# Gathered rows dealt to the sixteen partition sets in one unbroken count, with the half-loaded batch among them

## The chip, the core and the metric

The kernel runs on one core of a Trainium2 chip. Five engines of the core work side by side: TensorE (PE, with its weight loads shown as PEld), VectorE (DVE), ScalarE (ACT), GpSimd (POOL) and SyncE (SP). Each takes its instructions in program order, and waits on semaphores for the others. Data moves between the device's memory and the on-chip memory by DMA: a transfer over 128 partitions is spread over sixteen DMA engines. The metric is device time in microseconds (us); less is better.

## What is computed

For each of 32 batches, 128 rows of 1024 floats are picked out of 512 by an index list:

```python
x:       (32, 512, 1024) float32
indices: (32, 128) int32, values 0..511
for b in range(batch):
    result[b] = x[b, indices[b]]
```

The indices are drawn from a fixed seed. A batch names between 109 and 120 different rows with its 128 indices; the rest are repeats. A row is 4 KB, so the output is 16.8 MB, and reading every named row once would be about 14.9 MB.

## The kernel before

A batch can go one of three ways to the output.

**Direct batches.** The first HEAD = 4 batches are gathered as they are: one indirect DMA on POOL's queue fetches row indices[b, p] into partition p of a block (repeats are read again), and a store on SP's queue writes the block out. TensorE takes no part. The loop over range(HEAD) issues them, after the columns of indices have been turned upright (idxT, by one product of vf with ident).

**Sparse batches.** Batches 5 to 31 are read without repeats. For each, the kernel finds which of the 128 positions are the first with their value, numbers these, gives each number a partition, and fetches only these rows into a buffer of the ring held (RING = 8 buffers u0 to u7, zeroed by ScalarE at the start). Entries that get no row point beyond the batch and are skipped by the bounds check. A product with a 0/1 matrix (spread[b]) then copies the fetched rows to all the positions that want them, in two halves of 512 columns (spread_rows); ScalarE copies the halves from PSUM to the block, and SP stores it. When TensorE is done with a buffer, the gather for eight batches later is issued to it (fetch).

The index work is done for GROUP = 3 batches at once, in three steps:
- step0 (lines 166 to 175): a product spreads each batch's values over all partitions (bc); VectorE counts for each position the earlier positions with the same value (cnt) and marks those with none (lead).
- step1 (177 to 187): a product of lead with the triangle above counts the leaders before each position (rk, then nth). An exclusive-or with shift, which is the batch's number modulo 16, changes which sets get the odd rows. The result, made unusable for non-leaders by 256 x cnt, is compared with turn to give the matrix pack.
- step2 (189 to 198): a product with pack puts each leader's index on its partition (at, the table that the gather reads), and a comparison with bc gives the spreading matrix.

turn comes from rank, which is laid out so that the low four bits of a number name one of sixteen sets of eight neighbouring partitions. Thus a batch with 112 + r different rows gives each set seven rows, and r of the sets an eighth.

**The half-loaded batch.** Batch 4 (HALF) has its rows 0 to 255 loaded whole at the start by two plain DMAs on ScalarE's queue (early). Only its indices from 256 up are gathered, each at its own position and with repeats (half_index), into ring buffer u0. half_spread makes its own bc and three matrices: one for each early tile and the identity for u0. half_rows adds the products, the early ones in the opening and the last one when spread_rows(4) runs.

**Order.** Program order on PE, DVE and ACT is kept by the wrapper InOrder. In the opening come half_index and the fetch of batch 4; step0 of groups 0 and 1; then for four groups step1, step0 of the next group but one (for g = 1 and 2), step2, and the fetches of batches up to 11. half_spread stands behind group 0, and the early halves of half_rows behind groups 1 and 2. The main loop goes over batches 4 to 31: spread_rows, the fetch for eight batches on, and one step of the group four ahead. The gathers of POOL's queue are thus issued in batch order, and so are the stores of SP's.

Of the kernel before, what the change touches and what calls it, by code (L numbers as in the profile page):

```python
# [6 lines left out]
F32 = mybir.dt.float32  # L7
F16 = mybir.dt.float16
I32 = mybir.dt.int32
ALU = mybir.AluOpType  # L10
# [18 lines left out]
def kernel(ctx, tc, x, indices, out):  # L29
# [11 lines left out]

    nc = tc.nc
    B, S, D = x.shape
    N = indices.shape[1]
    HEAD, RING, GROUP, AHEAD, FAR = 4, 8, 3, 4, 1024
    HALF = HEAD
    PAIRED = range(12, 20)  # L50
    SPARSE = HEAD + 1
    GROUPS = (B - SPARSE) // GROUP
    assert 2 * N <= S <= FAR and (B - SPARSE) % GROUP == 0
    const = ctx.enter_context(tc.tile_pool(name="const", bufs=1))
    ring = ctx.enter_context(tc.tile_pool(name="ring", bufs=1))
    rows = ctx.enter_context(tc.tile_pool(name="rows", bufs=1))
    pick = ctx.enter_context(tc.tile_pool(name="pick", bufs=1))
    junkp = ctx.enter_context(tc.tile_pool(name="junk", bufs=4))
    PS = bass.MemoryType.PSUM
    pbc = ctx.enter_context(tc.tile_pool(name="pbc", bufs=2, space=PS))  # L60
    psm = ctx.enter_context(tc.tile_pool(name="psm", bufs=1, space=PS))
    pout = ctx.enter_context(tc.tile_pool(name="pout", bufs=4, space=PS))
    pe, dve, act = InOrder(tc), InOrder(tc), InOrder(tc)
    mm, v = nc.tensor.matmul, nc.vector
# [8 lines left out]
    diff = const.tile([N, N], I32, name="diff")  # L73
    nc.gpsimd.iota(diff[:], pattern=[[1, N]], base=0, channel_multiplier=-1)
    rank = const.tile([N, 8, 16], I32, name="rank")
    for e in range(8):
# [2 lines left out]
            fold ^= col * (e >> bit & 1)  # L79
        steps = [[(-16 if fold >> bit & 1 else 16) << bit, 2] for bit in (2, 1, 0)]  # L80
        nc.gpsimd.iota(rank[:, e], pattern=[[1, 2]] + steps, base=2 * e + 16 * fold, channel_multiplier=0)
    shift = const.tile([N, 2, 16], I32, name="shift")
    nc.gpsimd.iota(shift[:], pattern=[[0, 2], [1, 16]], base=0, channel_multiplier=0)
    shift = shift[:].rearrange("p t s -> p (t s)")

    zero = const.tile([N, 1], F32, name="zero")
    dve(v.memset, zero[:], 0.0)
    ident = const.tile([N, B], F16, name="ident")
# [2 lines left out]
    dve(v.tensor_scalar, out=below[:], in0=diff[:], scalar1=0, scalar2=None, op0=ALU.is_lt)  # L91
    above = const.tile([N, N], F16, name="above")
    dve(v.tensor_scalar, out=above[:], in0=diff[:], scalar1=0, scalar2=None, op0=ALU.is_gt)
    turn = const.tile([N, N], F16, name="turn")
    dve(v.tensor_copy, out=turn[:], in_=rank[:].rearrange("p e q -> p (e q)"))
    vf = const.tile([N, N], F16, name="vf")
    dve(v.memset, vf[:], 0.0)
    dve(v.tensor_copy, out=vf[:B],
        in_=vals[:].bitcast(I32).rearrange("p (n two) -> p n two", two=2)[:, :, 0])
# [3 lines left out]
    early = [rows.tile([N, D], F32, name=f"early{k}") for k in range(2)]  # L103
# [10 lines left out]
    idxT = const.tile([N, B], I32, name="idxT")  # L114
    dve(v.tensor_copy, out=idxT[:], in_=tr[:])
    idxF = const.tile([N, B], F32, name="idxF")
# [6 lines left out]
    def gather(dst, at, b, **kw):  # L123
        nc.gpsimd.indirect_dma_start(  # L124
            out=dst, out_offset=None,
            in_=xf[:], in_offset=bass.IndirectOffsetOnAxis(ap=at, axis=0),
            element_offset=b * S * D, **kw)
# [22 lines left out]
    def table(name, dtype):  # L150
        return const.tile([N, B], dtype, name=name)

    cnt, lead, slot = table("cnt", F32), table("lead", F16), table("slot", F16)
    nth, at = table("nth", I32), table("at", I32)
    bcs, packs, spread = {}, {}, {}

    def of_group(g):
        return range(SPARSE + g * GROUP, SPARSE + (g + 1) * GROUP)

    def cols(t, g):  # L160
        return t[:, SPARSE + g * GROUP:SPARSE + (g + 1) * GROUP]

    def wide(t):
        return t.rearrange("p (g o) -> p g o", o=1).to_broadcast([N, GROUP, N])

    def step0(g):

        bcs[g] = bc = pbc.tile([N, 4, N], F32, name="bc")
        for k, b in enumerate(of_group(g)):
            pe(mm, bc[:, k], lhsT=ident[:, b:b + 1].to_broadcast([N, N]), rhs=vf[:], start=True, stop=True)  # L170
        for k, b in enumerate(of_group(g)):
            junk = junkp.tile([N, N], F16, name="junk")
            dve(v.scalar_tensor_tensor, out=junk[:], in0=bc[:, k], scalar=idxF[:, b:b + 1], in1=below[:],
                op0=ALU.is_equal, op1=ALU.mult, accum_out=cnt[:, b:b + 1])
        dve(v.tensor_scalar, out=cols(lead, g), in0=cols(cnt, g), scalar1=0.0, scalar2=None, op0=ALU.is_equal)

    def step1(g):

        rk = psm.tile([N, GROUP], F32, name="rk")
        pe(mm, rk[:], lhsT=above[:], rhs=cols(lead, g), start=True, stop=True)  # L180
        dve(v.tensor_copy, out=cols(nth, g), in_=rk[:])
        dve(v.tensor_tensor, out=cols(nth, g), in0=cols(nth, g), in1=cols(shift, g), op=ALU.bitwise_xor)
        dve(v.scalar_tensor_tensor, out=cols(slot, g), in0=cols(cnt, g), scalar=256.0, in1=cols(nth, g),
            op0=ALU.mult, op1=ALU.add)
        packs[g] = pack = junkp.tile([N, GROUP, N], F16, name="pack")
        dve(v.tensor_tensor, out=pack[:], in0=turn[:].rearrange("p (o n) -> p o n", o=1).to_broadcast([N, GROUP, N]),
            in1=wide(cols(slot, g)), op=ALU.is_equal)

    def step2(g):

        pos = psm.tile([N, GROUP], F32, name="pos")
        for k, b in enumerate(of_group(g)):
            pe(mm, pos[:, k:k + 1], lhsT=packs[g][:, k], rhs=near[:, b:b + 1], start=True, stop=True)
        dve(v.tensor_scalar, out=cols(at, g), in0=pos[:], scalar1=float(FAR), scalar2=None, op0=ALU.add)
        s = pick.tile([N, GROUP, N], F32, name=f"s{g}")
        dve(v.tensor_tensor, out=s[:], in0=bcs[g][:, :GROUP], in1=wide(cols(at, g)), op=ALU.is_equal)
        for k, b in enumerate(of_group(g)):
            spread[b] = s[:, k]

    def fetch(b):  # L200
        if HEAD <= b < B:
            gather(held[(b - HEAD) % RING][:], at[:, b:b + 1], b, bounds_check=S - 1, oob_is_err=False)

    held = []
# [2 lines left out]
        act(nc.scalar.copy, out=u[:], in_=zero[:].to_broadcast([N, D]))  # L207
        held.append(u)

    def half_index():  # L210

        c = slice(HALF, HALF + 1)
        dve(v.tensor_scalar, out=nth[:, c], in0=idxT[:, c], scalar1=2 * N, scalar2=FAR,
            op0=ALU.is_lt, op1=ALU.mult)
        dve(v.tensor_tensor, out=at[:, c], in0=nth[:, c], in1=idxT[:, c], op=ALU.add)

    def half_spread():

        less = const.tile([N, 1], F32, name="less")
        dve(v.tensor_copy, out=less[:], in_=diff[:, 0:1])  # L220
        bc = pbc.tile([N, 4, N], F32, name="bc")
        pe(mm, bc[:, 0], lhsT=ident[:, HALF:HALF + 1].to_broadcast([N, N]), rhs=vf[:], start=True, stop=True)
        same = pick.tile([N, 3, N], F32, name="same")
        for k in range(2):
            dve(v.tensor_scalar, out=same[:, k], in0=bc[:, 0], scalar1=less[:], scalar2=float(k * N),
                op0=ALU.add, op1=ALU.is_equal)
        dve(v.tensor_scalar, out=same[:, 2], in0=diff[:], scalar1=0, scalar2=None, op0=ALU.is_equal)
        spread[HALF] = same

    def half_rows(h, last):  # L230
        w = slice(h * 512, (h + 1) * 512)
        if not last:
            spread[HALF, h] = pout.tile([N, 512], F32, name="ps")
        ps, same = spread[HALF, h], spread[HALF]
        for k in ((2,) if last else (0, 1)):
            pe(mm, ps[:], lhsT=same[:, k], rhs=(early + held[:1])[k][:, w], start=k == 0, stop=k == 2)
        if last:
            nc.scalar.copy(out=blocks[HALF][:, w], in_=ps[:])  # L238

    def spread_rows(b):  # L240
        for h in range(2):
            if b == HALF:
                half_rows(h, True)
                continue
            w = slice(h * 512, (h + 1) * 512)
            ps = pout.tile([N, 512], F32, name="ps")
            pe(mm, ps[:], lhsT=spread[b], rhs=held[(b - HEAD) % RING][:, w], start=True, stop=True)
            nc.scalar.copy(out=blocks[b][:, w], in_=ps[:])  # L248
        store(b)

    half_index()
    fetch(HALF)
    step0(0)
    step0(1)
    for g in range(AHEAD):
        step1(g)
        if 0 < g < AHEAD - 1:
            step0(g + 1)
        step2(g)
        for b in of_group(g):  # L260
            if b < HEAD + RING:
                fetch(b)
        if g == 0:
            half_spread()
        elif g < 3:
            half_rows(g - 1, False)
    for b in range(HEAD, B):
        spread_rows(b)
        fetch(b + RING)
        g, step = divmod(b - SPARSE, GROUP)  # L270
        if b >= SPARSE and g + AHEAD < GROUPS:
            (step0, step1, step2)[step](g + AHEAD)


# [28 lines left out]
```

## Time and profile before

| | |
|---|---|
| median of 5 runs | 88.29 us (87.72 to 88.64) |
| the profiled execution | 89.93 us, of which the span is 88.1 us |
| busy in the span: PE / ACT / POOL / DVE | 63.0 / 41.8 / 33.8 / 27.5 us |
| DMA traffic | 32.86 MB, mean 373 GB/s |
| queue of POOL (gathers) | 14.96 MB |
| queue of SP (index loads and stores) | 16.81 MB |
| queue of ACT (early) | 1.05 MB |
| gathers to blocks / to the ring | 4 / 28 |

The span is the time from the first to the last instruction of one profiled execution. The page cuts it into 40 slices of 2.2 us and gives for each the busy share of every engine, the TensorE clock that was granted, the busy share of the DMA engines and what they moved. The chain of waits goes back from the last instruction to what released it, step by step. The timeline lists instructions with their start and duration, and in square brackets how long the engine had been idle and what ended that. A group such as "x4" is several instructions of one kind shown as one; a float32 product of 128x512 stands there as two matmuls. The time of a gather on POOL is that of issuing it; the rows land later. The trace also has the times at which the sixteen parts of a transfer report that they have landed (landing marks).

### The profile page before, as it was taken

The page shows a single profiled execution, that of the slowest core. Times are in us where ns is not written, and L with a number is a line of the kernel's source. Part 1 is how long each engine was busy: PE and PEld are TensorE (multiplying, and loading weights), DVE is VectorE, ACT ScalarE, POOL GpSimd, SP SyncE. Part 2 cuts the span into 40 slices and gives each one's busy share as a digit, 9 for nine tenths or more (in the row PEclk, how much of TensorE's full clock was granted, in tenths as well). Part 3 has the DMA queues.
Part 4 walks back from the last instruction along what each step waited for, and adds up shares of the span by engine and source line. Part 5 has one row for each costly group of instructions (what it writes and reads, how often), then busy time and mean ns, then how long its engine had stood idle before and what let it go on. Part 6 is the DMA issues. An engine that isn't in the chain of part 4 may idle for free.

```text
span 88.1 us, 801 instructions
## 1 busy us (share of the span) xinstructions
PE 63.0 (72%) x185; PEld 25.8 (29%) x185; DVE 27.5 (31%) x133; ACT 41.8 (47%) x65; POOL 33.8 (38%) x46
## 2 busy tenths in 40 slices
PE   0131379541999999999999999988868888887000
PEld 0120143211344354443454443333332222231000
DVE  2297890934304436645356463000000000000000
ACT  0999900000236666657657556645434555555000
POOL 7667877840035445665445655444400000000000
PEclk9999999999579999999999999999999999999955
DMA  0998989999988999999999999999999999999980
GB/s 0 264 405 281 268 324 413 415 417 422 417 353 270 305 389 420 415 417 413 405 420 418 418 417 418 418 424 418 418 418 418 420 418 417 417 420 420 424 348 13
DMA packets 9636, 32.86 MB, mean 373 GB/s; under 512 B 1597, under 2 KB 1629, under 8 KB 9632
## 3 DMA queue, kind: packets, MB, share of 16 engines
q1 hardware_dynamic: 4736, 16.81, 47.8%
q0 software_dynamic: 4608, 14.96, 44.0%
q10 hardware_dynamic: 288, 1.05, 3.1%
q8 instruction: 1, 0.02, 0.1%
q14 instruction: 3, 0.02, 0.1%
HBM read 17.86 MB, written 16.78 MB: 393 GB/s over the span
## 4 chain that ended last, share of the span: by engine, by line
PE 41%; DMA 22%; issue 11%; DVE 9%; POOL 5%; another core or an unknown queue 2%; ACT 1%; POOLq 1%; SPq 0%; DVEq 0%
PE ps L24 37%; DMA u<-in_x_dram,at 19%; POOL u L124 5%; DMA vals<-in_indices_dram 3%; PE pos L24 2%; DVE pack L24 2%; PE bc L24 2%; DVE junk L24 2%; DVE s L24 1%; DVE nth L24 1%; DVE same L24 1%; ACT block L248 1%; DVE at L24 1%; DVE slot L24 1%
## 5 line engine op out<-in xcount | busy, mean ns | idle before, releaser
L24 PE MATMUL ps<-u,s 128*128 128x512 f32 x108 | 51.4, 610 | 4.2 <-DMA u<-in_x_dram,at 3.5
L124 POOL DMA_INDIRECT u<-in_x_dram,at x28 | 28.1, 1002 | 26.7 <-PE ps L24 10.5
L248 ACT COPY block<-ps 128x512 f32<-128x512 f32 x38 | 22.3, 586 | 18.1 <-PE ps L24 17.0
L24 PEld LDWEIGHTS ps<-u,s 128*128 128x128 f32 x108 | 18.7, 192 | 28.3 <-ACT block L248 13.8
L248 ACT COPY pair<-ps 128x512 f32<-128x512 f32 x16 | 9.4, 586 | 5.7 <-PE ps L24 4.0
L24 DVE SCALAR_TENSOR_TENSOR junk<-bc,idxF,below 128x128 f16<-128x128 f32 x27 | 8.0, 347 | 9.6 <-PE bc L24 9.6
L238 ACT COPY block<-ps 128x512 f32<-128x512 f32 x2 | 1.2, 586 | 13.7 <-PE ps L24 13.7
L24 ACT COPY u<-zero 128x1024 f32<-128x1024 f32 x8 | 7.7, 1041 | 0.0
L24 PE MATMUL pos<-near,pack 128*128 128x1 f16 x27 | 2.0, 167 | 6.8 <-DVE pack L24 5.7
L24 PE MATMUL ps<-early,same 128*128 128x512 f32 x8 | 5.7, 847 | 0.0
L24 PEld LDWEIGHTS <-pack 128*128 128x128 f16 x27 | 1.7, 99 | 12.1 <-DVE pack L24 8.9
L24 DVE TENSOR_TENSOR pack<-turn,slot 128x384 f16<-128x384 f16 x9 | 5.0, 558 | 0.3
L24 DVE TENSOR_TENSOR s<-bc,at 128x384 f32<-128x384 f32 x9 | 5.0, 558 | 0.3
L24 PE MATMUL bc<-vf,ident 128*128 128x128 f16 x28 | 3.5, 247 | 1.5 <-DVE at L24 0.8
L24 DVE CAST nth<-rk 128x3 int32<-128x3 f32 x9 | 1.4, 160 | 7.9 <-PE rk L24 3.5
L24 PEld LDWEIGHTS <-ident 128*128 128x128 f16 x28 | 2.5, 110 | 4.3 <-issue 4.3
L24 PE MATMUL ps<-u,same 128*128 128x512 f32 x4 | 3.6, 1061 | 0.0
L124 POOL DMA_INDIRECT block<-in_x_dram,idxT x3 | 2.9, 950 | 1.6 <-DVE nth L24 1.0
L21 PE MATMUL pos<-ident,vf 128*128 128x32 f16 x1 | 0.2, 210 | 4.2 <-DVE vf L24 4.2
L24 DVE TENSOR_SCALAR at<-pos 128x3 int32<-128x3 f32 x9 | 1.4, 161 | 4.0 <-PE pos L24 4.0
L24 PE MATMUL rk<-lead,above 128*128 128x3 f16 x9 | 1.6, 172 | 1.1 <-issue 1.1
L24 ACT ACT_TABLE_LOAD x1 | 1.3, 1283 | 2.2 <-DVE ident L24 2.2
(31 smaller groups left out, 17.2 us busy)
## 6 DMA issues: line engine op xcount, KB each, us to landing
out_dram<-block SPq DMA_DIRECT2D x24, 512.0 KB
out_dram<-pair SPq DMA_DIRECT2D x4, 1024.0 KB
early<-in_x_dram ACTq DMA_DIRECT2D x2, 512.0 KB
u<-in_x_dram,at POOLq DMA_INDIRECT x28
block<-in_x_dram,idxT POOLq DMA_INDIRECT x3
vals<-in_indices_dram SPq DMA_DIRECT2D x1, 32.0 KB
first<-in_indices_dram SPq DMA_DIRECT2D x1, 1.0 KB
block<-in_x_dram,first POOLq DMA_INDIRECT x1
```

Source lines behind the costliest of these rows:

```text
L21: self.last = do(*args, **kw)
L24: self.last = do(*args, **kw)
L124: nc.gpsimd.indirect_dma_start(out=dst, out_offset=None, in_=xf[:], in_offset=bass.IndirectOffsetOnAxis(ap=at, axis=0), element_offset=b * ...
L238: nc.scalar.copy(out=blocks[HALF][:, w], in_=ps[:])
L248: nc.scalar.copy(out=blocks[b][:, w], in_=ps[:])
```

## The change

The number of direct batches goes from four to five. The half-loaded batch becomes batch 5, the first of the sparse batches, and goes through step0 to step2 like the others: a comparison adds one to cnt for indices below 256, so that these positions are no leaders, and its own index step and identity matrix go. Groups now cover batches 5 to 31 including it; their number, nine, stays.

In place of the exclusive-or with the batch's number, the count of leaders runs on from batch to batch. past holds for each position the number of earlier sparse batches in which it led (one addition per batch at the end of step0), and a second product, with the all-ones matrix every, adds the sum of past over the positions to rk. The number is then taken modulo 128.

```diff
-    HEAD, RING, GROUP, AHEAD, FAR = 4, 8, 3, 4, 1024
+    HEAD, RING, GROUP, AHEAD, FAR = 5, 8, 3, 4, 1024
     HALF = HEAD
     PAIRED = range(12, 20)
-    SPARSE = HEAD + 1
-    GROUPS = (B - SPARSE) // GROUP
-    assert 2 * N <= S <= FAR and (B - SPARSE) % GROUP == 0
+    GROUPS = (B - HEAD) // GROUP
+    assert 2 * N <= S <= FAR and (B - HEAD) % GROUP == 0
...
-    shift = const.tile([N, 2, 16], I32, name="shift")
-    nc.gpsimd.iota(shift[:], pattern=[[0, 2], [1, 16]], base=0, channel_multiplier=0)
-    shift = shift[:].rearrange("p t s -> p (t s)")
-
+    less = const.tile([N, 1], F32, name="less")
...
+    dve(v.tensor_copy, out=less[:], in_=diff[:, 0:1])
+    every = const.tile([N, N], F16, name="every")
+    dve(v.memset, every[:], 1.0)
...
+    past = const.tile([N, B + 1], F16, name="past")
+    dve(v.memset, past[:, HEAD:HEAD + 1], 0.0)
...
+        if HALF in of_group(g):
+            c = slice(HALF, HALF + 1)
+            dve(v.scalar_tensor_tensor, out=cnt[:, c], in0=idxF[:, c], scalar=2.0 * N, in1=cnt[:, c],
+                op0=ALU.is_lt, op1=ALU.add)
         dve(v.tensor_scalar, out=cols(lead, g), in0=cols(cnt, g), scalar1=0.0, scalar2=None, op0=ALU.is_equal)
+        for b in of_group(g):
+            dve(v.tensor_tensor, out=past[:, b + 1:b + 2], in0=past[:, b:b + 1], in1=lead[:, b:b + 1], op=ALU.add)
...
-        pe(mm, rk[:], lhsT=above[:], rhs=cols(lead, g), start=True, stop=True)
+        pe(mm, rk[:], lhsT=above[:], rhs=cols(lead, g), start=True, stop=False)
+        pe(mm, rk[:], lhsT=every[:], rhs=cols(past, g), start=False, stop=True)
         dve(v.tensor_copy, out=cols(nth, g), in_=rk[:])
-        dve(v.tensor_tensor, out=cols(nth, g), in0=cols(nth, g), in1=cols(shift, g), op=ALU.bitwise_xor)
+        dve(v.tensor_scalar, out=cols(nth, g), in0=cols(nth, g), scalar1=N - 1, scalar2=None, op0=ALU.bitwise_and)
...
-    def half_index():
-
-        c = slice(HALF, HALF + 1)
-        dve(v.tensor_scalar, out=nth[:, c], in0=idxT[:, c], scalar1=2 * N, scalar2=FAR,
-            op0=ALU.is_lt, op1=ALU.mult)
-        dve(v.tensor_tensor, out=at[:, c], in0=nth[:, c], in1=idxT[:, c], op=ALU.add)
-
     def half_spread():
 
-        less = const.tile([N, 1], F32, name="less")
-        dve(v.tensor_copy, out=less[:], in_=diff[:, 0:1])
-        bc = pbc.tile([N, 4, N], F32, name="bc")
-        pe(mm, bc[:, 0], lhsT=ident[:, HALF:HALF + 1].to_broadcast([N, N]), rhs=vf[:], start=True, stop=True)
-        same = pick.tile([N, 3, N], F32, name="same")
+        same = pick.tile([N, 2, N], F32, name="same")
         for k in range(2):
-            dve(v.tensor_scalar, out=same[:, k], in0=bc[:, 0], scalar1=less[:], scalar2=float(k * N),
+            dve(v.tensor_scalar, out=same[:, k], in0=bcs[0][:, HALF - HEAD], scalar1=less[:], scalar2=float(k * N),
                 op0=ALU.add, op1=ALU.is_equal)
-        dve(v.tensor_scalar, out=same[:, 2], in0=diff[:], scalar1=0, scalar2=None, op0=ALU.is_equal)
-        spread[HALF] = same
+        spread[HALF, "early"] = [same[:, k] for k in range(2)]
...
+        if last:
+            pe(mm, ps[:], lhsT=spread[HALF], rhs=held[(HALF - HEAD) % RING][:, w], start=False, stop=True)
+        else:
+            for k in range(2):
+                pe(mm, ps[:], lhsT=spread[HALF, "early"][k], rhs=early[k][:, w], start=k == 0, stop=False)
...
-    half_index()
-    fetch(HALF)
     step0(0)
     step0(1)
...
-        g, step = divmod(b - SPARSE, GROUP)
-        if b >= SPARSE and g + AHEAD < GROUPS:
+        g, step = divmod(b - HEAD, GROUP)
+        if g + AHEAD < GROUPS:
             (step0, step1, step2)[step](g + AHEAD)
```

Where SPARSE stood in of_group and cols, HEAD now stands.

More of the change, by code (lines that the diff above doesn't have):

```diff
@@ L154 @@
     nth, at = table("nth", I32), table("at", I32)
+    past = const.tile([N, B + 1], F16, name="past")
+    dve(v.memset, past[:, HEAD:HEAD + 1], 0.0)
     bcs, packs, spread = {}, {}, {}
     def of_group(g):
-        return range(SPARSE + g * GROUP, SPARSE + (g + 1) * GROUP)
+        return range(HEAD + g * GROUP, HEAD + (g + 1) * GROUP)
     def cols(t, g):
-        return t[:, SPARSE + g * GROUP:SPARSE + (g + 1) * GROUP]
+        return t[:, HEAD + g * GROUP:HEAD + (g + 1) * GROUP]
     def wide(t):
@@ L233, in half_rows @@
             spread[HALF, h] = pout.tile([N, 512], F32, name="ps")
-        ps, same = spread[HALF, h], spread[HALF]
-        for k in ((2,) if last else (0, 1)):
-            pe(mm, ps[:], lhsT=same[:, k], rhs=(early + held[:1])[k][:, w], start=k == 0, stop=k == 2)
+        ps = spread[HALF, h]
+        if last:
[3 more added lines that the diff above has]
+                pe(mm, ps[:], lhsT=spread[HALF, "early"][k], rhs=early[k][:, w], start=k == 0, stop=False)
         if last:
```

## The prediction

> **What bounds the kernel now.** I read the page's slices first: they tell whether an engine or the transfers set the end.
>
> ```profile
> PEclk9999999999579999999999999999999999999955
> DMA  0998989999988999999999999999999999999980
> GB/s 0 264 405 281 268 324 413 415 417 422 417 353 270 305 389 420 415 417 413 405 420 418 418 417 418 418 424 418 418 418 418 420 418 417 417 420 420 424 348 13
> ```
>
> From the sixteenth slice to the last but two the transfers move some 418 GB/s without a break. That is 102 rows of 4 KB in a microsecond (418,000 / 4096), and it is the bound: the time is the rows to be moved divided by that rate, plus what is lost where the rate sinks. It sinks twice, in slices 4 to 6 and in slices 12 to 15. The chain of waits agrees: its last long link is a gather that took 16.66 us to land because rows stood in front of it.
>
> ```profile
> 61.91 0.23 POOLq L298
> 62.13 16.66 DMA u<-in_x_dram,at
> 78.80 0.14 issue
> 78.93 1.97 PE ps L24 x4
> ```
>
> Next I cut the span into stretches (columns: stretch, length, busy time and count for each engine, clock, DMA share, GB/s).
>
> ```profile
> 22.00:24.20 2.20, 2.20 (x3) 0.84 (x3) 0.72 (x2) 0.41 (x1) 0.00 (x0) 0.50 1.03 417
> 24.20:26.40 2.20, 2.20 (x5) 0.97 (x4) 0.00 (x0) 0.78 (x3) 0.67 (x1) 0.73 0.89 361
> 26.40:28.60 2.20, 2.20 (x9) 0.94 (x8) 1.07 (x7) 1.43 (x3) 1.33 (x2) 1.00 0.90 268
> 28.60:30.80 2.20, 2.20 (x7) 0.82 (x6) 1.08 (x4) 1.48 (x3) 1.00 (x1) 1.00 0.90 304
> 30.80:33.00 2.20, 2.20 (x12) 1.15 (x11) 0.72 (x2) 1.29 (x3) 1.00 (x1) 1.00 1.01 389
> 33.00:35.20 2.20, 2.20 (x8) 0.91 (x7) 1.38 (x9) 1.43 (x3) 1.14 (x2) 1.00 1.02 413
> ```
>
> Against 418 GB/s, 24.2 to 35.2 us lacks (57 + 150 + 114 + 29 + 5) x 2.2 = 781 KB, or **1.87 us** of transfer: the hole. The timeline tells why.
>
> ```profile
> 11.63 3.70 PE L24 MATMUL ps<-early,same 128*128 128x512 f32 x4
> ...
> 16.70 1.96 PE L24 MATMUL ps<-early,same 128*128 128x512 f32 x4
> ...
> 18.55 1.00 POOL L124 DMA_INDIRECT u<-in_x_dram,at  x1 [0.98 <-issue]
> ...
> 20.52 0.16 DVE L24 CAST nth<-rk 128x3 int32<-128x3 f32 x1 [2.15 <-remote]
> ...
> 21.82 2.78 PE L24 MATMUL ps<-u,same 128*128 128x512 f32 x3
> ```
>
> ```profile
> 25.73 1.00 POOL L124 DMA_INDIRECT u<-in_x_dram,at  x1 [6.18 <-PE ps L24]
> ```
>
> The ring's eighth gather is issued at 18.55; the ninth must wait until TensorE has used up the first buffer, and comes at 25.73, 6.18 us after POOL went idle. Four direct stores have landed by 22.5 (landing marks of the trace). So the work that needs no TensorE result runs out at about 26 us, before TensorE has delivered blocks to store and buffers to refill.
>
> **Cover that the change adds.** I counted rows in the reference's seeded inputs; batches 5 to 12 have 117, 112, 115, 114, 116, 111, 119, 117 distinct values, and batch 4 has 58 indices from 256 up. Before: 4 x 128 direct, 256 early, 58 half, and batches 5 to 11 (804) are 1630 rows of reads, with 4 x 128 of stores. After: 5 x 128 direct, 256 early, 60 for batch 5 (its distinct values from 256 up), and batches 6 to 12 (804) are 1760, with 5 x 128 of stores. That is 258 rows more ahead of TensorE's first delivery: **2.53 us** at 102 a microsecond. The kernel's whole count goes from 3651 gathered rows (the page's 14.96 MB of the software queue agrees) to 3664, only 13 more; so the rest is work moved forward into the hole.
>
> **What the added steps cost in the opening.** All VectorE work is in program order, so each operation pushes what is behind it. Two spacings from the timeline: operations that don't need each other start 0.10 us apart (4.43, 4.54, 4.64), and those that do, 0.20 us (nth 7.27, slot 7.47, pack 7.67).
> - The moved copy into less and the ones in every fall in VectorE's wait for vals (idle 1.27 us before 3.91): nothing. Without that cover, 0.2 us.
> - Out go the two half-index operations (junk starts at 5.01 instead of 4.73: 0.28); in comes one memset of past (0.10): -0.18.
> - First group: one operation for the half batch and three sums, each needing the last, 4 x 0.20: +0.80. Second group, three sums: +0.60. Both stand ahead of the first nth, so it and the first index table come 1.22 us later (8.72 to 9.94). POOL's own spacing of 1.31 would let it take batch 5 at 9.97; a waiting gather starts some 0.77 us after its table (at 17.78, issue 18.55), so about 10.7. Direct rows are queued then (landing marks of the fourth gather: 13.4 to 14.7), which hides that.
> - The half batch's own bc, the wait on it and the third same go (s ends at 9.32, next nth at 10.33: 1.01; two same at 0.27 are left): -0.50. Shift 0.72 at the first early matmuls.
> - rk is two matmuls now. One more 128x3 with its load is about 0.10 (bc loads start 0.10 apart); two lie on the path, of groups 2 and 3. The sums of group 2 run while TensorE does the early matmuls, and group 3's do likewise. Shift **0.85 us** at the first rows of the ring: 21.82 to about 22.7. Group 3's sums do delay the table of group 2: batch 11 is issued at about 19.9 and batch 12 at 21.2, still far ahead of the end of the backlog.
> - Behind it, each group has 0.6 us more VectorE work and one more matmul for three batches. Blocks leave TensorE every 1.88 us there (the chain shows 5.65 for three) against 2.35 that the transfers need (the last gathers and stores are 2.3 to 2.4 apart): 1.4 us of slack a group. Nothing; were that cover gone, 0.1 us a group, five groups.
> - POOL loses the shift table (0.15) in front of a gather that waits for first: nothing.
>
> The early matmuls are unchanged. Their speed matters, as TensorE's start rests on them. **A rule against a row:** the Trainium skill, "TensorE: Matmul & The Clock Gate", Part 1, has the array at half clock until it has been busy for some 3.4 us, and back there after such an idle window. The page's clock row is full for the second four (1.96 us for the four), which would end them at 18.66; but nth, which needs the product behind them, starts only at 20.52. So these four took 3.7 us, like the first (3.56 from 11.77). By the rule a longer pause could cool an array that is warm; by the trace it is slow here already, and my pause grows by 0.1 us. I take 0; were the second four warm at present and cooled by the change, 1.8 us.
>
> **Sum.** Cover 2.53 less delay 0.85 is 1.68 us, of a hole of 1.87. I take 1.5: the sixteen queues won't run dry together. Were first delivery and cover to miss each other it would be nearer 1.0; the top is 1.87.
>
> **Balance.** Counted over sets of eight partitions, the rows of a set range from 225 to 231 before; after, every set has 229. A row costs 0.157 us on its queue. The last store's sixteen landing marks show fifteen between 85.4 and 86.4 us, which is six rows, and one alone at 87.2; one queue has been that far behind the others since the instruction loads (the page's q8 and q14) at 41.3. It sets the end, and it isn't one of the two sets with 225, as both lowest marks are there. Between 231 to 229 (-0.31) and 226 to 229 (+0.47), I take 0, near the middle of the sets. More instructions might bring one more load, +0.3; loads on other queues would give back 0.7. **Another rule against the change:** "DMA: Bandwidth & Descriptors", The descriptor swizzle, gives a queue two runs of four partitions, not eight neighbours, so the deal would miss the queues. Counted by that formula the spread is 226 to 232 before and 229 everywhere after: the order inside the sets makes both agree, and the sum stands. The same page (Bandwidth) has HBM transfers held at 358 GB/s for a core; then no hole could be won back. The slices hold 418, so the rows decide.
>
> In the profiled execution (89.93 us, span 88.1) this gives a span of 86.6. The runs' median, 88.29, is 1.64 below that execution; taken from it, 88.29 - 1.5 = **86.8 us**.
>
> **Rivals.**
> 1. *The fifth direct gather meets the first hole.* Slices 4 to 6 move 291 GB/s, 71 rows a microsecond, though rows are queued. If direct gathers are slow by nature, 128 more cost 128/71 - 128/102 = 0.55 us, leaving 87.3 to 87.5. For: the slow slices are those of the direct gathers. Against: the fourth's rows land from 13.4 to 14.7 us, when the rate is back at 413. Chance 0.14.
> 2. *The cover is eaten.* POOL's late tables or TensorE's start slip by 2 us and only the balance shows: 88.0 to 88.5. Chance 0.12.
> 3. *The index chain becomes the bound (slower).* The sums stand in a row on VectorE, four groups of three, with early matmuls waiting in order behind their groups. The deciding point is TensorE's first ring rows at 21.82 + 2.53 = 24.35 us; each microsecond beyond lengthens the run by one. With sums at 0.45 each instead of 0.20 (a dependent step next to another engine's can take 0.26 already), twelve add 3.0 us if all lie on the path: start 25.7, time 89.6. Against: half of them lie beside the early matmuls. Chance 0.12.
> That the deal does nothing is inside the first sum, which takes nothing for it.
>
> **How the numbers follow.** The forecast has 0.62, with a range of its own of 86.2 to 87.3. Reaching to the rivals leaves 85.9 to 88.5, which drops the slow end. What a measurement of this kernel tells from no change is about 0.5%, 0.44 us. Faster: the forecast, and most of rival 1, 0.74. Same: the rest of it and most of rival 2, 0.13. Slower: rival 3 and a little of rival 2, 0.13.
>
> **What would show it.** Slices 12 to 15 at 400 or more; ring rows on TensorE at 22.7; batch 12's gather near 21, and the next near 26.6; first sparse gather near 10.7; fifteen of the last landing marks within 0.3 us. DVE has 160 operations, PE 193. It is wrong if the hole is there as before, if ring rows start after 24.3, or if slices 4 to 6 spread to a seventh.

## The result and the profile after

| | median | lowest to highest | executions |
|---|---|---|---|
| before | 88.64 us | 87.72 to 90.56 | 79 |
| after | 88.27 us | 87.67 to 89.31 | 42 |

Ratio 0.9976, 95% interval 0.9961 to 0.9992: 0.2 us faster, which is less than a measurement of this kernel can tell from no change. The forecast was 86.8 us. The ratio leaves out every execution that took over 1.5% longer than the best of its kernel, and the profile of before that the prediction was worked from is of such an execution (89.93 us, against a median of 88.64). Over all executions the medians are 0.37 us apart, and 21 of 79 took more than 89 us before, 1 of 42 after.

The page of the changed kernel has a span of 86.3 us in an execution of 88.06. The slices that the prediction named:

```profile
PEclk9999999999999999999999999999999999999965
DMA  0897999999999999999999999999999999999980
GB/s 0 289 405 218 255 348 406 416 420 418 418 418 422 422 414 414 424 418 416 405 420 424 416 420 416 420 425 416 418 418 418 424 414 420 416 422 424 414 359 15
```

Slices 12 to 15, which moved 353, 270, 305 and 389 GB/s, now move 414 to 422: the second hole is gone. Slices 4 to 6 are as low as before. The same in stretches (stretch, length, busy time and count of PE, PEld, DVE, ACT and POOL; then clock, DMA share, GB/s):

```profile
22.00:24.20 2.20, 1.95 (x9) 0.91 (x10) 0.91 (x3) 0.59 (x1) 0.00 (x0) 1.00 1.04 423
24.20:26.40 2.20, 2.20 (x11) 1.15 (x10) 1.61 (x11) 1.29 (x3) 1.00 (x1) 1.00 1.03 417
26.40:28.60 2.20, 2.20 (x9) 0.91 (x9) 1.36 (x6) 1.50 (x3) 1.21 (x2) 1.00 1.03 421
28.60:30.80 2.20, 2.20 (x9) 1.03 (x8) 0.96 (x6) 1.31 (x3) 1.32 (x2) 1.00 1.02 417
30.80:33.00 2.20, 2.20 (x8) 1.02 (x7) 1.82 (x12) 1.18 (x3) 1.26 (x2) 1.00 1.03 421
```

And the gathers around TensorE's first delivery, POOL's timeline:

```profile
19.45 1.00 POOL L122 DMA_INDIRECT u<-in_x_dram,at  x1 [1.47 <-issue]
20.75 1.00 POOL L122 DMA_INDIRECT u<-in_x_dram,at  x1 [0.31 <-issue]
24.57 1.00 POOL L122 DMA_INDIRECT u<-in_x_dram,at  x1 [2.82 <-PE bc L24]
```

Batch 12 is fetched at 20.75, ahead of TensorE's first delivery, as forecast (21.2). The first refill comes at 24.57, where 26.6 was forecast (bc, named in its row, is what TensorE runs next to its last product with that buffer). The span fell by 1.8 us from one profile to the other, slightly more than the 1.5 that the sum gave. Yet the times hardly moved. So either the hole was not there in most executions of the kernel before (theory A), or it was, and the gain from filling it was given back elsewhere (theory B).

### The profile page after: what moved, and what is told of

The parts are those of the page before. It is cut to its first block, busy times and chain, and to the rows that moved or that the text cites. A ratio compares the mean times of both kernels' runs of the same rounds, so it can differ in the third digit from the quotient of the medians.

```text
span 86.3 us, 829 instructions
## 1 busy us (share of the span) xinstructions
PE 62.0 (72%) x189; PEld 25.5 (30%) x189; DVE 31.6 (37%) x160; ACT 40.6 (47%) x63; POOL 33.6 (39%) x45
## 4 chain that ended last, share of the span: by engine, by line
PE 42%; DMA 22%; issue 13%; DVE 8%; POOL 5%; ACT 1%; POOLq 1%; SPq 0%; DVEq 0%
PE ps L24 38%; DMA u<-in_x_dram,at 19%; POOL u L122 5%; DMA vals<-in_indices_dram 3%; DVE junk L24 2%; DVE pack L24 2%; PE bc L24 2%; PE pos L24 1%; DVE past L24 1%; DVE nth L24 1%; ACT block L246 1%; DVE slot L24 1%; SPq L66 0%; DVE lead L24 0%; PE rk L24 0%
## 5 line engine op out<-in xcount | busy, mean ns | idle before, releaser
L122 POOL DMA_INDIRECT u<-in_x_dram,at x27 | 27.0, 1000 | 24.3 <-PE bc L24 6.3
L246 ACT COPY block<-ps 128x512 f32<-128x512 f32 x36 | 21.1, 586 | 17.9 <-PE ps L24 16.8
L24 PE MATMUL ps<-early,same 128*128 128x512 f32 x8 | 7.5, 1096 | 0.0
L236 ACT COPY block<-ps 128x512 f32<-128x512 f32 x2 | 1.2, 586 | 12.6 <-PE ps L24 12.6
L24 DVE TENSOR_TENSOR past<-past,lead 128x1 f16<-128x1 f16 x27 | 4.4, 164 | 0.9
L122 POOL DMA_INDIRECT block<-in_x_dram,idxT x4 | 3.8, 950 | 1.7 <-issue 0.9
L24 PEld LDWEIGHTS ps<-early,same 128*128 128x128 f32 x8 | 2.4, 324 | 2.1 <-issue 2.1
```

What stands on the lines that cost most here:

```text
L24: self.last = do(*args, **kw)
L122: nc.gpsimd.indirect_dma_start(out=dst, out_offset=None, in_=xf[:], in_offset=bass.IndirectOffsetOnAxis(ap=at, axis=0), element_offset=b * ...
```

## Experiments

All ratios are to the kernel before, run beside them on the same chip.

**Was the hole always there?** The kernel before, with no edit, profiled again.

> The kernel before, unchanged, profiled once more. Theory A (the hole belonged to the execution that was profiled): TensorE is at full clock at 22 us, its first ring rows take about 1.9 us instead of 3.7, and 24.2 to 33 us moves more than 400 GB/s. Theory B (the hole is always there, the change fills it and gives it back elsewhere): 24.2 to 33 us lacks 1.5 us or more of transfer, as in the profile shown. Ratio 1.000 for both.

Its time is 88.75 us, ratio 1.0045 (1.0016 to 1.0074). As it is the same program, this says how far such a comparison can be off: nearly half a percent, more than its own interval tells. The profile, in stretches:

```profile
22.00:24.20 2.20, 2.20 (x6) 0.89 (x6) 0.00 (x0) 1.62 (x3) 1.00 (x1) 1.00 1.03 417
24.20:26.40 2.20, 2.20 (x10) 0.94 (x8) 1.08 (x7) 1.31 (x3) 1.00 (x1) 1.00 1.03 415
26.40:28.60 2.20, 2.20 (x10) 1.08 (x9) 1.24 (x5) 1.39 (x3) 1.00 (x1) 1.00 1.02 413
28.60:30.80 2.20, 2.20 (x9) 0.98 (x8) 0.93 (x4) 1.49 (x3) 1.30 (x2) 1.00 1.02 415
30.80:33.00 2.20, 2.20 (x8) 0.91 (x7) 1.36 (x9) 1.22 (x3) 1.26 (x2) 1.00 1.04 423
```

No hole in this one: theory A. What differs is TensorE. First the ScalarE copies of its first products in the profile that the prediction was made from, then those in this one:

```profile
23.79 0.59 ACT L238 COPY block<-ps 128x512 f32<-128x512 f32 x1 [12.62 <-PE ps L24]
25.49 0.59 ACT L238 COPY block<-ps 128x512 f32<-128x512 f32 x1 [1.12 <-PE ps L24]
```

```profile
22.04 0.58 ACT L238 COPY block<-ps 128x512 f32<-128x512 f32 x1 [10.88 <-PE ps L24]
22.89 0.58 ACT L238 COPY block<-ps 128x512 f32<-128x512 f32 x1 [0.27 <-PE ps L24]
```

In the first, half-products are 1.70 us apart, at a granted clock of 0.50 from 22.0 to 25.4. In the second they are 0.85 apart at 1.00, and the products also start earlier, at 20.89 instead of 21.82. The first block is complete 2.6 us earlier, POOL's ninth ring gather comes at 23.13 instead of 25.73, and the backlog lasts until then. The spans are 88.1 and 86.6 us: 1.5 us, for a hole that was worked out at 1.87.

**The two halves of the change apart.** Five direct batches with the old numbering, as an edit to the changed kernel (`...` stands for lines left out):

```diff
...
-        pe(mm, rk[:], lhsT=every[:], rhs=cols(past, g), start=False, stop=True)
-        dve(v.tensor_scalar, out=cols(nth, g), ... scalar1=N - 1, op0=ALU.bitwise_and)
+        dve(v.tensor_tensor, out=cols(nth, g), in0=cols(nth, g), in1=cols(shift, g), op=ALU.bitwise_xor)
```

> Five direct batches and the half-loaded batch among the groups, but the numbering with the exclusive-or as before: the 258 rows of cover without the sums on VectorE. Theory A: nothing to fill, ratio 0.997 to 1.002 (88.3 to 88.8 us). Theory B: the cover without its price, more than 1 us faster, ratio 0.985 to 0.990.

Measured 1.0047 (1.0001 to 1.0092), outside theory A's range by 0.27 points, and 1.5 points from theory B's. The cover alone gains nothing here; over all 14 executions the median is even 89.48 us, against 88.34 beside it. Its profile fell on an execution with a low clock for twice as long, and shows where the cover ends:

```profile
22.00:24.20 2.20, 1.10 (x5) 0.59 (x6) 1.66 (x6) 0.00 (x0) 0.00 (x0) 0.55 1.04 425
24.20:26.40 2.20, 2.20 (x4) 0.82 (x3) 0.00 (x0) 0.58 (x1) 0.00 (x0) 0.50 1.03 417
26.40:28.60 2.20, 2.20 (x6) 1.10 (x5) 1.07 (x7) 0.58 (x1) 1.00 (x1) 0.50 1.01 410
28.60:30.80 2.20, 2.20 (x7) 0.86 (x6) 0.64 (x4) 1.17 (x2) 0.54 (x1) 0.90 0.99 350
...
33.00:35.20 2.20, 2.20 (x9) 0.99 (x8) 1.07 (x7) 1.43 (x3) 1.08 (x2) 1.00 0.91 246
```

With the clock near 0.5 until 28.6 us the first products come at 25.29 and 26.99, and a hole opens at 28.6 instead of 24.2.

The numbering alone, on four direct batches, as an edit to the kernel before:

```diff
...
+        for b in of_group(g):
+            dve(v.tensor_tensor, out=past[:, b + 1:b + 2], in0=past[:, b:b + 1], in1=lead[:, b:b + 1], op=ALU.add)
...
+        pe(mm, rk[:], lhsT=every[:], rhs=cols(past, g), start=False, stop=True)
-        dve(v.tensor_tensor, out=cols(nth, g), in0=cols(nth, g), in1=cols(shift, g), op=ALU.bitwise_xor)
+        dve(v.tensor_scalar, out=cols(nth, g), ... scalar1=N - 1, op0=ALU.bitwise_and)
```

> The unbroken count alone, with four direct batches and the half-loaded batch apart, as before: the sums and the second product without the cover. Theory A: the longer index chain (about 0.9 us at TensorE's first ring rows) is hidden by the backlog in most executions, ratio 0.995 to 1.002. Theory B: the chain costs what it is late, 0.9 us, ratio 1.008 to 1.012.

Measured 0.9987 (0.9963 to 1.0012): theory A. In its profile the first ring rows start at 21.47 us, later than the 20.89 of e1, and the stretches from 22 to 33 us hold 412 GB/s or more. So in the executions that the ratio compares the longer index chain costs nothing. But 9 of its 22 took more than 89 us, against 6 of 51 of the kernel before beside it, and the means are 0.4 us apart (88.82 and 88.42): that it is free without the cover is not shown.

**A hole made on purpose.** In both kernels, ahead of the main loop:

```diff
+    for k in range(4):
+        idle = pout.tile([N, 512], F32, name="ps")
+        pe(mm, idle[:], lhsT=early[k % 2][:, :N], rhs=early[k % 2][:, :512], start=True, stop=True)
     for b in range(HEAD, B):
```

> The kernel before with four float32 products of 128x512 (8 matmuls, 3.4 us at full clock), whose result nobody reads, put on TensorE ahead of the first ring rows: the delay that a slow clock made in the profile shown, in every execution. Theory A (a hole is there only when TensorE is late, and then costs what the backlog does not cover): about 1.5 to 3 us slower, ratio 1.017 to 1.035. Theory B (the hole was there in all executions already): 3 us and more, ratio 1.035 to 1.045.

> The same four products in the same place of the changed kernel. Theory A: the 258 rows of cover take up 2.5 us less what the longer chain uses, so it stays within 1 us of the changed kernel, 88.3 to 89.4 us, 1.3 us or more below the kernel before with the same delay. Theory B (the cover is eaten elsewhere): as late as that one, within 0.5 us of it.

> The changed kernel, unchanged, on the same chip and with the same runs of the kernel before as its late twin. Both theories: ratio 0.995 to 1.000; its profile has no hole between 22 and 35 us.

| | median | ratio | 95% interval |
|---|---|---|---|
| before, late | 89.93 us | 1.0195 | 1.0161 to 1.0228 |
| after, late | 88.61 us | 1.0022 | 0.9997 to 1.0046 |
| after | 88.47 us | 1.0008 | 0.9981 to 1.0034 |

The first two are as theory A has it, and the third is 0.08 points outside the range that both had, well inside its interval. The late kernel before, then the late changed one:

```profile
24.20:26.40 2.20, 2.20 (x6) 0.95 (x6) 0.00 (x0) 1.21 (x3) 0.67 (x1) 1.00 0.99 400
26.40:28.60 2.20, 2.20 (x9) 0.96 (x8) 1.07 (x7) 1.43 (x3) 1.33 (x2) 1.00 0.92 296
28.60:30.80 2.20, 2.20 (x8) 0.82 (x7) 1.08 (x4) 1.45 (x3) 1.00 (x1) 1.00 0.95 305
30.80:33.00 2.20, 2.20 (x12) 1.15 (x11) 0.72 (x2) 1.31 (x3) 1.00 (x1) 1.00 1.01 395
```

```profile
24.20:26.40 2.20, 2.20 (x9) 0.91 (x8) 0.00 (x0) 0.58 (x1) 0.00 (x0) 1.00 1.03 417
26.40:28.60 2.20, 2.20 (x11) 1.09 (x8) 1.72 (x11) 1.39 (x3) 1.00 (x1) 1.00 1.02 415
28.60:30.80 2.20, 2.20 (x9) 0.97 (x8) 1.36 (x6) 1.49 (x3) 1.30 (x2) 1.00 1.02 378
30.80:33.00 2.20, 2.20 (x9) 0.93 (x8) 0.96 (x6) 1.22 (x3) 1.32 (x2) 1.00 1.03 412
```

From 24.2 to 33 us the first lacks (18 + 122 + 113 + 23) x 2.2 = 607 KB, 1.45 us at 418 GB/s, and the medians are 1.48 us apart (89.93 against 88.45; 1.7 by the ratio): the loss of transfer and the loss of time agree. On the medians the same delay costs the changed kernel 0.14 us. But 8 of its 22 late executions took more than 89 us, against 1 of 22 without the delay, and on the means the delay costs 0.5 us (88.95 against 88.46). So the cover does most of what the sum said, and the median execution does not need it.

Is it the cover that makes executions over 89 us rare in the changed kernel? That is not shown. In all of its runs the mean granted clock of an execution was 0.972 or more, where that of the kernel before went down to 0.95; TensorE may simply not have been slow.

The opposite, TensorE woken up early by 42 small products, missed its purpose.

```diff
+    def warm(n):
+        idle = pout.tile([N, 512], F32, name="ps")
+        for _ in range(n):
+            pe(mm, idle[:, :N], lhsT=below[:], rhs=below[:], start=True, stop=True)
     step0(1)
+    warm(18)
```

(and warm(8) after step1 of groups 0 and 1 and after step2 of group 0)

> The kernel before with 42 products of 128x128 that nobody reads in TensorE's idle time from 5 to 11 us, so that it is at full clock for the early matmuls (0.43 us instead of 0.86 each) and reaches its first ring rows some 2 us or more earlier in every execution. Theory A (in most executions no hole is left to fill): ratio 0.995 to 1.002. Theory B (a hole of more than 1 us is still in most executions): ratio 0.982 to 0.989.

Ratio 1.0119 (1.0018 to 1.022), from six executions. The early matmuls started at 13.85 us instead of 11.51 (e1), still 0.85 us apart, and the first ring rows at 24.13: the products stood in the way and did not raise the clock. It is one more late TensorE, and it says nothing on theory A.

**Does the balance of the sets matter?** In the changed kernel:

```diff
-        pe(mm, rk[:], lhsT=above[:], rhs=cols(lead, g), start=True, stop=False)
-        pe(mm, rk[:], lhsT=every[:], rhs=cols(past, g), start=False, stop=True)
+        pe(mm, rk[:], lhsT=above[:], rhs=cols(lead, g), start=True, stop=True)
```

> The changed kernel with each batch numbered from 0 (the second product left out): every batch gives its odd rows to the first sets, so that the fullest set has 242 gathered rows in all and the emptiest 218, against 229 in each. Theory R (the fullest queue sets the end, 0.157 us a row): 13 rows, 2.0 us slower than the changed kernel, ratio 1.018 to 1.026. Theory S (what a queue loses in the opening and to instruction loads decides, and a few rows vanish in it): under 1 us, ratio 1.003 to 1.012.

Measured 89.52 us, ratio 1.0138 (1.005 to 1.0226); against the changed kernel's 1.0008 that is 1.3%, 1.1 us. It lies between the two theories, and with four executions its interval reaches into both: 13 rows more in the fullest set cost about half of what 0.157 us a row gives. The end of the page's GB/s row shows the one-sided finish, 351, 118, 11 in the last three slices where the changed kernel has 414, 359, 15. So an uneven deal does cost, but the 2 rows between the fullest set before (231) and after (229) would be 0.2 us by this measure.

**The first hole.** It is in every profile: 2.7 to 3.0 us of transfer are lacking between 2.2 and 13.2 us in the two profiles of each kernel. Is ScalarE's zeroing of the ring to blame? In the changed kernel half of it went to VectorE:

```diff
...
+        if k >= 4:
+            dve(v.memset, u[:], 0.0)
...
-        act(nc.scalar.copy, out=u[:], in_=zero[:].to_broadcast([N, D]))
```

> The changed kernel with the last four ring buffers zeroed by VectorE while it waits for the indices, ScalarE zeroing the first four only (its copies end near 7.7 us instead of 11.2). Theory Z (ScalarE's zeroing slows the transfers of the opening): the stretch 7.7 to 12 us moves 400 GB/s, about 1.2 us faster, ratio 0.985 to 0.989. Theory Q (the slow stretch belongs to gathers that run alone or are fresh in the queue): the stretch stays at 220 to 340 GB/s, ratio 0.995 to 1.005.

Ratio 1.0216 (1.0172 to 1.0259). Each memset took 0.91 us, and the four held VectorE until 6.93, so that the second gather went out at 7.76 us instead of 4.86. ScalarE's copies ended at 7.38. The timeline's windows after that:

```profile
8.80:9.90 1.10, 0.33 (x2) 0.10 (x1) 1.00 (x7) 0.00 (x0) 0.88 (x1) 1.00 1.04 410
9.90:11.00 1.10, 0.00 (x0) 0.00 (x0) 0.96 (x9) 0.00 (x0) 0.80 (x2) 1.00 0.68 93
11.00:13.20 2.20, 0.29 (x5) 0.24 (x6) 1.73 (x8) 0.00 (x0) 1.16 (x2) 1.00 0.95 359
```

The 410 GB/s are the store of the first direct block, on SP's queue. Then next to nothing moves: the rows of the second gather, issued at 7.76, start at 10.2. Gathers alone then move 359 GB/s, and 302 from 13.2 to 15.4 us. Theory Z falls on these two figures: ScalarE is idle throughout (0.00, the fourth column of pairs), and gathers are as far from 418 as in the other profiles. Theory Q missed the ratio: the late table made the run long.

Are the repeated rows of direct batches to blame? Again in the changed kernel:

```diff
...
+    dve(v.tensor_scalar, out=zeros[:], in0=idxT[:, :HEAD], scalar1=0, scalar2=None, op0=ALU.mult)
+    dve(v.scalar_tensor_tensor, out=spaced[:], in0=diff[:, 0:1].to_broadcast([N, HEAD]), scalar=-4.0,
+        in1=zeros[:], op0=ALU.mult, op1=ALU.add)
...
-        gather(blocks[b], ... idxT[:, b:b + 1], b)
+        gather(blocks[b], ... spaced[:, b:b + 1], b)
```

> The changed kernel with direct batches 1 to 4 fetching rows 0, 4, 8 ... 508 of their batch in place of the rows that the indices name, so that no row is read twice (their output is then not the reference's); the table still waits for idxT, some 0.3 us longer. Theory D (repeated rows make the direct gathers of the opening slow): 6.6 to 13.2 us moves 380 GB/s or more, 1 us faster or better, ratio under 0.990. Theory N (repeats have nothing to do with it): that stretch stays between 230 and 340 GB/s, ratio 0.997 to 1.006.

The stretches from 6.6 to 13.2 us move 244, 192 and 322 GB/s, none near theory D's 380 and one below theory N's 230: theory D falls. The ratio, 1.011 (1.0082 to 1.0139), was expected by neither. The two operations made the table later than meant: the second gather goes out at 5.47 us instead of 4.86, and by the ratios the run is 1.0%, 0.9 us, behind the changed kernel. By 13.2 us it has started to move the bytes of 771 rows, the changed kernel of 833 and 843 (its two profiles). A late gather in the opening is paid for.

**An earlier opening.** Then an early one should pay. The index table is loaded on a second queue, beside the column that the first gather waits for:

```diff
-    nc.sync.dma_start(out=vals[:], in_=indices)
+    act(nc.scalar.dma_start, out=vals[:], in_=indices)
```

> The changed kernel with the whole index table (vals) loaded over ScalarE's queue, beside the column first on SyncE's, instead of behind it: idxT and the second gather come 0.4 us earlier. Theory O (the gathers of the opening are on the path, as a later table suggests): 0.3 to 0.6 us faster than the changed kernel, ratio to the kernel before 0.991 to 0.997. Theory P (only late gathers cost, early ones gain nothing): ratio 0.997 to 1.003.

Measured 87.81 us against 88.68, ratio 0.994 (0.9903 to 0.9978): faster than the kernel before. By the ratios of the changed kernel (0.9976 and 1.0008) it is 0.4 to 0.7% below that one too, about as much as such comparisons can be off. POOL's second gather, in the changed kernel and here:

```profile
4.79 0.95 POOL L122 DMA_INDIRECT block<-in_x_dram,idxT  x1 [0.82 <-DVE past L24]
```

```profile
4.28 0.95 POOL L122 DMA_INDIRECT block<-in_x_dram,idxT  x1 [0.30 <-DVE junk L24]
```

It now comes as soon as POOL is done with the first. By 33 us the kernel has moved 2871 rows, the changed one 2853 and 2841, which is 0.2 to 0.3 us; and its last sixteen marks lie between 83.4 and 84.7 us, with none alone behind. Why none is, was not tried. Does the gain need the change? The same edit to the kernel before:

> The same move of vals to ScalarE's queue in the kernel before. Theory O (earlier gathers shorten the opening, whatever the deal): as much as in the changed kernel, ratio 0.991 to 0.997. Theory P (the gain needed the changed kernel's cover): ratio 0.997 to 1.003.

Ratio 0.9964 (0.9932 to 0.9996): in theory O's range, though its interval reaches into the other. But 11 of the 22 executions took more than 89 us (8 of 27 of the kernel before beside them), and over all of them the median is 88.97 us, against 88.52. With the change none of 12 took more than 88.5, though seven had a mean granted clock of 0.946 to 0.963. The profile here is of an execution of ordinary length, 88.86 us, and yet it has a hole:

```profile
PEclk9999999996599999999999999999999999999995
GB/s 15 311 395 275 307 352 390 420 416 418 420 401 241 369 416 418 420 416 416 420 416 422 414 418 420 416 418 420 420 418 420 420 420 418 420 420 422 422 305 19
```

The granted clock is 0.50 from 20.3 to 23.7 us, and from 24.2 to 30.8 some 1.2 us of transfer are lacking. Such a hole takes back more than the earlier opening gains. That the cover is what keeps e11 short is likely, and not shown: where in its executions the clock was low is known for the profiled one alone.

## Why the prediction was wrong

- **The step that failed** is the last line of the sum: "The runs' median, 88.29, is 1.64 below that execution; taken from it, 88.29 - 1.5 = 86.8 us". The profiled execution was 1.64 us longer than the median, and the hole I meant to win back was worth 1.5 to 1.87 us. That is the same time, counted twice: an execution near the median had no such hole to win back. e1's profile (88.38 us) has none, and e4 makes the hole again at 1.48 us. The span of the changed kernel was forecast at 86.6 us and found at 86.3, but that agreement is luck: the kernel before has 86.6 without any change when TensorE is in time (e1), as it was in the profile after.
- **The cover** (258 rows, 2.53 us, less the later start) is right in kind, and is measured by e4 and e5: a delay that costs the kernel before 1.48 us costs the changed one 0.14 on the medians and 0.5 on the means.
- **The clock.** I said of the early matmuls that TensorE "is slow here already", and took its half speed at the first ring rows as given too. The Trainium skill, "TensorE: Matmul & The Clock Gate", Part 1, says that the window of this gate runs free of the kernel, so that the turning point differs from run to run. The profiles agree: the first ring rows run at 0.50 in one execution of the kernel before and at 1.00 in another, and where the granted clock fell in mid-kernel it did so for 3.4 us (before, e12) or for twice that (e2). I had weighed that section for a longer pause and not for this.
- **The opening's steps** were priced too high: ring rows were forecast 0.85 us later (22.7) and start at 22.34. The operation of the half batch starts without a pause behind the last count, and the two same operations no longer wait for a bc of their own. The first sparse gather, forecast at 10.7, goes out at 10.45. By 13.2 us the changed kernel has moved 833 and 843 rows of 4 KB (its two profiles), the kernel before 860 (e1) and 839 (the profile before), so whether the rearranged opening gives back anything, 0.2 us at most, can't be told; the 13 rows more are 0.13 us.
- **The balance**, taken as 0, was about right for the time and wrong in what it rests on. I read the 1.0 us between fifteen landing marks as six rows. With 229 rows in every set they still spread over 1.2 us in the profile after (83.5 to 84.7), and fourteen over 1.3 in the other (83.6 to 84.9), where 0.3 was forecast. So the counts of rows don't make that spread; what does was not tried. One mark at 85.36 still stands alone in the first profile, two at 85.45 and 85.55 in the other. The limit of 358 GB/s that the prediction took from the Trainium skill, "DMA: Bandwidth & Descriptors", Bandwidth, is there the share of a core when both cores of a pair run; for one core alone, as here, that section has up to 425, and the slices show 418.
- **Rivals.** The second comes nearest in time (88.0 to 88.5), for another reason. The first is answered in part: e10 keeps the low rates without repeated rows, and the seventh slice moves 406 and 370 GB/s in the two profiles of the changed kernel, 413 and 392 in those of the kernel before. The third did not come: the ring rows start at 22.34, well ahead of 24.35.

## What to carry to other kernels

When the profiled execution is longer than the median by about as much as the loss you mean to remove, look first whether the loss is that difference: profile again, or look at the clock row in the stretch. A cover is tested by making the thing it covers late in both kernels; that shows its worth even where the ordinary time does not move. Count the long executions too: a cover for a delay that not every execution has can show in them and not in the median. And where transfers bound the middle and the end, as here, look for time where the queue is still dry, at the first transfers.

## What the runs showed of the hardware

TensorE's completion reports can come later than its records suggest. In e1 a small product (pos) stands at 16.6 to 16.8 us, but its semaphore moves at 18.91, and that of the four early matmuls behind it, recorded until 18.6, at 18.98. In e2 the same matmuls are recorded until 18.1 and report at 21.83. In both, the clock record had gone to full a little before (16.2 and 15.4 us); but in e4, where it did at 14.8, the same products report within 0.02 us of their recorded ends (16.9 and 18.7). So TensorE's speed is better read from who waits for it than from its own rows. The cause stays open.

From 6.6 to 13.2 us gathers and the first stores move 60 to 75% of the rate that is reached later on. The same queue, with gathers issued some microseconds earlier, moves 413 of the 417 GB/s of 24.2 to 26.4 us in the changed kernel, where next to no store is under way. A gather's packet of 4 KB takes 0.21 and 0.24 us in its stretches from 6.6 to 8.8 and 8.8 to 11 us, at a DMA share of 0.81 and 0.99, and 0.13 from 24.2 to 26.4: in the opening the DMA engines are mostly busy, with slower packets. Neither ScalarE's writes (e6) nor repeated rows (e10) make the difference; what does is not settled.
